# Other queues for three of a stage's stores, and products written over the keys: one step of a hybrid decoder on one core

## The chip, the cores and the metric

The kernel runs on one core of a Trainium2 chip. The time is device microseconds of one execution. Engines are TensorE, VectorE, ScalarE, GpSimd and SyncE; in profile rows they are PE (PEld for its weight loads), DVE, ACT, POOL and SP. A name with a q behind it, as SPq, is the sequencer of that engine, which issues DMAs and waits.

## The reference

One layer for a prompt of 2048 tokens and for 8 samples of 4 new tokens each. The input is normalised and multiplied by one wide matrix; half of the result goes through attention, half through an mLSTM; both are gated and meet in an output matrix. What matters here is the attention of the new tokens, which see a cache of 2048 keys and values per sample in three patterns:

```python
DILATED_PATTERNS = ((128, 1), (512, 4), (2048, 16))      # window, step

def dilated_partial_sample(q, kc, vc, dil, n_back):
    idx = WB + jnp.arange(T)[:, None] - jnp.arange(n_back + 1)[None, :] * dil
    kg, vg = jnp.take(kc, idx, axis=1), jnp.take(vc, idx, axis=1)
    s = jnp.einsum('bthe,btjhe->bthj', q, kg) * (HEAD_DIM_ATT ** -0.5)
    ...
    return m, den, acc
```

and, of the prompt, the rotated keys and the values, which are outputs as they are (`p_win_k`, `p_win_v`), and the queries, keys and values that its own attention reads.

## The kernel before

The work is in three stages. The first projects the prompt, the second runs the prompt's attention from what the first has stored in DRAM (`q_scr`, `k_scr`, `v_scr`), the third runs the mLSTM and the output matrix. The change lies in the first (`phase_a`).

There the prompt is cut in 16 tiles of 128 tokens. For each tile `unit(i, j)` runs five projections of 512 columns: j = 0 queries, 1 keys, 2 values, 3 and 4 gates. Each is 24 matmuls of 128x512 (L165 to L167) into one PSUM tile of four; then ScalarE and VectorE take it out: for j < 3 as a high and a low 16-bit part (`t16`; the low part is L524), with the rotation of queries and keys on VectorE (L518 to L526) and GpSimd (L527 to L530), for keys and values also as 32-bit rows (`kvout`, L523); for the gates as `z` (L504, L505). All of it is stored: `t16` to `q_scr`, `k_scr` or `v_scr` (L533), `kvout` to `p_win_k` or `p_win_v` (L535), `z` to `z_scr` (L506). All these stores are issued by SyncE, as are the loads.

The first four tiles run projection by projection, as the weights come in. From the fifth on, tile by tile, other work is mixed in by its place in the program: preparing later weights (L134 to L148), normalising the next tokens (L215 to L226, stored as `x_scr` by GpSimd, L492), and the samples' attention. Its scores (`SampleAttention.scores`, one call for each of the 8 samples, spread over tiles 4 to 10 by the tuple `SCORES`) go without TensorE: the sample's four queries are replicated over 128 partitions in the tile `d_qb` (one buffer, L372), and for each pattern a = 2, 1, 0 a tile of keys `d_kv` (two buffers) is loaded (L366; L362 for a = 0, which needs one key per partition for all four tokens). For a = 2 and 1 GpSimd multiplies the queries into the key tile (L379), four products of 128x512; for a = 0 VectorE multiplies the keys into the query tile (L381). VectorE reduces each product (L382). After the eighth sample come a softmax (its sum is L401) and the values (L428) on TensorE; their key tiles use the same two buffers, and `d_qb`.

The order on each engine, and on each queue, isn't written out: a planner lays it out at build time from the program's order and a simulated time. An engine runs its instructions in that order, and a wait holds all behind it.

Of the kernel before, what the change touches and what calls it, by code (L numbers as in the profile page):

```python
# [16 lines left out]
ALU = mybir.AluOpType  # L17
# [13 lines left out]
NTOK = 4  # L31
# [122 lines left out]
def token_matmuls(nc, ps, x16, tok, hi, lo, cols):  # L154

    for last in token_steps(nc, ps, x16, tok, hi, lo, cols):
        pass
    return last
# [120 lines left out]
class SampleAttention:  # L279
# [89 lines left out]
    def scores(self, b):  # L369
        G, nc = self.G, self.G.nc  # L370
        qb = self.pool.tile([P, NTOK, 512], F32, tag="d_qb", name="d_qb")
        nc.sync.dma_start(out=qb.rearrange("p t e -> p (t e)"),  # L372
                          in_=G.ds_scr[0].rearrange("(b t) e -> b (t e)", t=NTOK)[b].partition_broadcast(P))
        for a in (2, 1, 0):
            t = self.piece("cache_win_k", b, a)
            for i in range(NTOK):
                p = t[:, i] if a else qb[:, i]
                if a:
                    nc.gpsimd.tensor_tensor(p, p, qb[:, i], ALU.mult)  # L379
                else:  # L380
                    nc.vector.tensor_tensor(p, p, t[:, 0], ALU.mult)  # L381
                nc.vector.tensor_reduce(self.sc[:, a, b, i], p.rearrange("p (h d) -> p h d", d=DA), AX.X, ALU.add)  # L382

    def softmax(self):
# [72 lines left out]
def phase_a(G, I, O):  # L457

    nc, tc = G.nc, G.tc
    wv = I["w_in"].rearrange("(kt p) c -> p kt c", p=P)  # L460
    wo = I["w_out"].rearrange("(kt p) c -> p kt c", p=P)
    with ExitStack() as st:
# [32 lines left out]
        def unit(i, j):  # L495

            x16 = x16s[i // 2]
            tok = slice((i % 2) * P, (i % 2 + 1) * P)
            rows = slice(i * P, (i + 1) * P)
            ps = pp.tile([P, 512], F32, tag="proj", name="ps_proj", bufs=4)  # L500
            pe = token_matmuls(nc, ps, x16, tok, hi[j], lo[j], slice(0, 512))
            if j >= 3:
                z = pool.tile([P, 512], F32, tag="z", name="z", bufs=2)
                nc.scalar.activation(z, ps, AF.Tanh, scale=G.whinv[:, j:j + 1])  # L504
                nc.vector.scalar_tensor_tensor(z, z, 1.0, ps, ALU.add, ALU.mult)  # L505
                nc.sync.dma_start(out=G.z_scr[rows, (j - 3) * 512:(j - 2) * 512], in_=z)  # L506
                return pe
            pv = ps.rearrange("p (h d) -> p h d", d=DA)
            R = 0 if j == 2 else 16
            t16 = v16[i % 2] if j == 2 else pool.tile([P, HA, (2 * DA, 3 * DA)[j]], F16, tag="t16", name="t16", bufs=3)  # L510
            l0 = 66 if j == 2 else DA
            o = pool.tile([P, HA, DA], F32, tag="kvout", name="kvout", bufs=2) if j else None
            if j < 2:
                ra = pool.tile([P, HA, 16], F32, tag="ra", name="ra")
                rb = pool.tile([P, HA, 16], F32, tag="rb", name="rb")
                r = pool.tile([P, HA, 16], F32, tag="rr", name="rr", bufs=2)
                table = lambda c, n: G.rope_p[:, i, c:c + n].unsqueeze(1).broadcast_to([P, HA, n])
                nc.vector.tensor_tensor(ra, pv[:, :, 0:16], table(0, 16), ALU.mult)  # L518
                two = lambda x: x.rearrange("p h (a e) -> p h a e", a=2)
                nc.vector.tensor_tensor(two(rb), two(pv[:, :, 0:16])[:, :, ::-1], two(table(16, 16)), ALU.mult)  # L520
            nc.scalar.activation(t16[:, :, R:DA], pv[:, :, R:], AF.Copy, scale=USC)
            if j:
                nc.scalar.activation(o[:, :, R:], pv[:, :, R:], AF.Copy, scale=G.wainv[:, j:j + 1])  # L523
            nc.vector.scalar_tensor_tensor(t16[:, :, l0 + R:l0 + DA], pv[:, :, R:], USC, t16[:, :, R:DA], ALU.mult, ALU.subtract)  # L524
            if j < 2:
                nc.vector.tensor_tensor(r, ra, rb, ALU.add)  # L526
                nc.gpsimd.tensor_copy(t16[:, :, 0:16], r)  # L527
                nc.gpsimd.tensor_tensor(t16[:, :, DA:DA + 16], r, t16[:, :, 0:16], ALU.subtract)
            if j == 1:
                nc.gpsimd.tensor_scalar(o[:, :, 0:16], r, G.isc[:, 1:2], 0.0, ALU.mult, ALU.add)  # L530
                nc.scalar.activation(t16[:, :, 2 * DA:], t16[:, :, 0:DA], AF.Copy)
            scr = (G.q_scr, G.k_scr, G.v_scr)[j]
            nc.sync.dma_start(out=scr.rearrange("r t e -> t r e")[rows], in_=t16.rearrange("p (r h) e -> p r (h e)", r=4))  # L533
            if j:
                nc.sync.dma_start(out=O["p_win_k" if j == 1 else "p_win_v"][rows, :], in_=o.rearrange("p h d -> p (h d)"))  # L535
            return pe

        def gate_unit(i):
# [43 lines left out]
        for j in range(5):  # L582
            if j < 3:
                wf.append(w_load(j + 2))
            if 0 < j < 4:
                if j == 1:
                    with tc.issue_after(last[DVE]):
                        prepare(j + 1, wf[j + 1])
                else:
                    prepare(j + 1, wf[j + 1])  # L590
            if j == 4:
                weights(G, pool, ginv, weight_loads(G, pool, wv[:, :, 4608:4616], 8), 8, G.gcol, sb=wg)
                xs = pool.tile([P, KT, NS], F32, tag="xs", name="xs")
                nc.sync.dma_start(out=xs, in_=I["xsT"].rearrange("(kt p) t -> p kt t", p=P))
                norm_columns(G, pool, pp, xs, G.xd.rearrange("p k a t -> p a k t"), NS, pool.tile([P, 4, NS], F32, tag="sq2s", name="sq2"), tag="s")
            for i in range(4):
                unit(i, j)
                if j == 4:
                    gate_unit(i)
                    if i == 1:  # L600
                        run(xprep(2))
# [24 lines left out]
        for i in range(4, NT):  # L626
            block = blocks.get(i)
            if block is not None:
                next(block)
            if i % 2 == 0 and i // 2 + 1 < 8:  # L630
                norm = xprep(i // 2 + 1)
                next(norm)
            for j in range(5 if i < NT - LATE else 3):
                pe = unit(i, j)
                if pending is not None and j == 1:
                    behind(pe, pending)
                    pending = None
                if block is not None and j in (0, 3 if i < NT - LATE else 2):
                    behind(pe, block)
                if j == 1 and i // 2 + 1 < 8:  # L640
                    behind(pe, norm)
            gate_unit(i)
            pending = block
            for _ in range(SCORES.count(i)):
                SA.scores(b_next["k"])
                b_next["k"] += 1
            if i == SCORES[-1]:
                SA.softmax()
            for _ in range(VALUES.count(i)):
                SA.values(b_next["v"])  # L650
                b_next["v"] += 1
            if i == VALUES[-1]:
                SA.finish()
# [8 lines left out]
        for n, (i, j) in enumerate(late):  # L662
            unit(i, j)
            if n == 2:
                stacks(G, 0, G.stk, lambda: pp.tile([P, 512], F32, tag="proj", name="ps_k", bufs=4).bitcast(F16))
# [1057 lines left out]
```

## Time and profile before

| | |
|---|---|
| median of 3 runs | 1520.45 us (1520.35 to 1530.15) |
| profiled execution | 1522.74 us |
| its span | 1520.6 us |
| TensorE busy | 1383.7 us (91%) |
| VectorE busy | 982.9 us (65%) |
| ScalarE busy | 737.2 us (48%) |
| GpSimd busy | 467.2 us (31%) |
| mean granted clock of TensorE | 0.97 |

The profile is of one execution. Its span goes from the first instruction to the last; the device time holds 2.1 us more. Matmuls overlap and their ends are modelled, so that a TensorE which is busy is not one at its peak; its idle time, though, is idle. The clock is a share of 2.4 GHz: 1 and 0.5 are its two levels, and a number between them is a mean.

### The profile page before, as it was taken

What the parts mean: (1) busy time and instruction counts of PE and PEld (TensorE: products, weight loads), DVE (VectorE), ACT (ScalarE), POOL (GpSimd) and SP (SyncE); (2) the same over time, 40 slices, a digit from 0 to 9 for tenths busy, and PEclk for the clock granted to TensorE, in tenths of its full rate; (3) what the DMA queues carried; (4) which work ended last, traced back from release to release, by engine and by line L of the source; (5) the groups of instructions that cost most, each with busy time, mean ns of one, the idle gap of its engine ahead of it and who ended that gap; (6) DMA issues with size and microseconds to landing.
All of it is one profiled execution on the core that took longest, in us unless ns stands there. A gap on an engine that the chain in (4) does not pass through costs nothing.

```text
span 1520.6 us, 28991 instructions
## 1 busy us (share of the span) xinstructions
PE 1383.7 (91%) x10679; PEld 856.3 (56%) x10679; DVE 982.9 (65%) x3054; ACT 737.2 (48%) x1685; POOL 467.2 (31%) x797
## 2 busy tenths in 40 slices
PE   4899988989999996999898976879999999999996
PEld 2445444444434346878688844555666666666653
DVE  5763776777643456888686804767666666666665
ACT  5365433454344336878687823334444444444432
POOL 1361334353310013645358932211211111111110
PEclk9999999999999998999999998989999999999999
DMA  8354587868869948977857866452655555553212
GB/s 295 111 181 159 164 279 289 280 217 308 278 213 379 324 136 288 340 220 227 237 173 208 306 234 213 149 174 74 212 160 188 160 187 160 188 160 106 78 48 77
DMA packets 153404, 310.96 MB, mean 204 GB/s; under 512 B 13533, under 2 KB 102782, under 8 KB 142686
## 3 DMA queue, kind: packets, MB, share of 16 engines
q1 hardware_dynamic: 149166, 230.10, 47.6%
q0 software_dynamic: 3952, 78.75, 14.2%
q8 instruction: 84, 1.38, 0.4%
q14 instruction: 58, 0.48, 0.1%
q10 hardware_dynamic: 144, 0.26, 0.0%
HBM read 231.80 MB, written 144.38 MB: 247 GB/s over the span
## 4 chain that ended last, share of the span: by engine, by line
PE 36%; DMA 19%; DVE 13%; ACT 5%; POOL 4%; issue 4%; SPq 1%; POOLq 0%; ACTq 0%; DVEq 0%
DMA Mb<-g_scr 5%; DMA qi<-g_scr 4%; PE ps_t L1052 3%; PE ps_proj L165 3%; PE ps_proj L167 3%; PE ps_proj L166 3%; DVE cd L1194 2%; DMA v<-v_scr 2%; PE ps_out L167 2%; PE ps_out L165 2%; PE ps_out L166 2%; DMA qn<-q_scr 2%; POOL d_kv L379 2%; PE ps_s L1030 2%; PE ps_dv L428 2%
## 5 line engine op out<-in xcount | busy, mean ns | idle before, releaser
L165 PE MATMUL ps_proj<-wa,x 128*128 128x512 f16 x640 | 246.2, 386 | 19.0 <-DVE t L524 10.1
L166 PE MATMUL ps_proj<-wa,x 128*128 128x512 f16 x640 | 246.5, 386 | 2.5 <-POOL wa L111 2.0
L167 PE MATMUL ps_proj<-wa,x 128*128 128x512 f16 x640 | 246.6, 386 | 1.0 <-ACT x L226 1.0
L1039 DVE CUSTOM_DVE_ANT_0 sc<-ps_s,mask,ncqk 128x256 f32<-128x256 f32 (+1 forms) x384 | 142.6, 420 | 25.7 <-PE ps_s L1031 9.0
L1041 POOL TENSOR_SCALAR sc<-sc,o 128x256 f32<-128x256 f32 (+1 forms) x272 | 113.0, 427 | 86.0 <-DVE o L1039 77.4
L165 PEld LDWEIGHTS <-x 128*128 128x128 f16 x768 | 73.8, 99 | 100.5 <-issue 16.9
L1056 DVE SCALAR_TENSOR_TENSOR tl<-ps_t,th 128x512 f16<-128x512 f32 (+1 forms) x152 | 102.4, 680 | 35.9 <-ACT th L1055 35.2
L167 PEld LDWEIGHTS <-x 128*128 128x128 f16 x768 | 73.4, 99 | 85.9 <-issue 12.9
L1194 DVE SCALAR_TENSOR_TENSOR cd<-pre,cw,cd 128x256 f32<-128x256 f32 x168 | 85.2, 512 | 51.9 <-ACT cd L1188 50.0
L166 PEld LDWEIGHTS <-x 128*128 128x128 f16 x768 | 73.4, 99 | 79.4 <-issue 11.4
L379 POOL TENSOR_TENSOR d_kv<-d_kv,d_qb 128x512 f32<-128x512 f32 x64 | 84.6, 1357 | 89.8 <-DMA d_qb<-ds_scr 80.5
L1055 ACT ACTIVATE th<-ps_t 128x512 f16<-128x512 f32 (+1 forms) x152 | 90.4, 595 | 37.2 <-PE ps_t L1052 35.3
L167 PE MATMUL ps_out<-wo,yt 128*128 128x512 f16 x256 | 95.5, 382 | 7.3 <-DVE yt L1291 6.4
L1052 PE MATMUL ps_t<-c_id,pr 128*128 128x128 f32 x600 | 100.3, 288 | 1.7 <-DVE tl L1056 1.4
L165 PE MATMUL ps_out<-wo,yt 128*128 128x512 f16 x256 | 98.0, 383 | 2.2 <-ACT yt L1293 1.1
L166 PE MATMUL ps_out<-wo,yt 128*128 128x512 f16 x256 | 97.8, 382 | 0.0
L1368 POOL TENSOR_TENSOR Mb<-Mb,big 128x512 f32<-128x512 f32 x16 | 20.3, 1269 | 250.1 <-DMA Mb<-g_scr 217.8
L1068 PE MATMUL ps_o<-v,th 128*128 128x65 f16 x600 | 80.6, 195 | 14.0 <-ACT th L1055 10.7
L1174 PE MATMUL ps_qk<-cx,wb 128*128 128x256 f16 x256 | 71.6, 280 | 17.9 <-ACT pre L1184 16.1
L1372 ACT ACTIVATE Mb<-Mb,gcols 128x128 f32<-128x128 f32 x64 | 20.5, 390 | 127.5 <-POOL Mb L1368 127.5
L1367 POOL TENSOR_TENSOR qi<-qi,qk 128x128 f32<-128x128 f32 x60 | 29.8, 523 | 162.9 <-DMA qi<-g_scr 149.0
L1069 PE MATMUL ps_o<-v,th 128*128 128x64 f16 x600 | 79.7, 196 | 0.0
(466 smaller groups left out, 3779.5 us busy)
## 6 DMA issues: line engine op xcount, KB each, us to landing
s_win_k<-cache_win_k POOLq DMA_DIRECT2D x32, 1022.0 KB, 8.2
s_win_v<-cache_win_v POOLq DMA_DIRECT2D x32, 1022.0 KB, 7.9
wf<-w_in SPq DMA_DIRECT2D x18, 1024.0 KB
d_kv<-cache_win_k SPq DMA_DIRECT2D x16, 1024.0 KB
d_kv<-cache_win_v SPq DMA_DIRECT2D x16, 1024.0 KB
A<-att_scr SPq DMA_DIRECT2D x16, 792.0 KB
w_scr<-wst SPq DMA_DIRECT2D x12, 1024.0 KB
att_scr<-o SPq DMA_DIRECT2D x9, 1056.0 KB
```

The source lines that it names most:

```text
L165: nc.tensor.matmul(ps, lhsT=xh, rhs=hi[:, kt, cols], start=kt == 0, stop=False)
L166: nc.tensor.matmul(ps, lhsT=xh, rhs=lo[:, kt, cols], start=False, stop=False)
L167: yield nc.tensor.matmul(ps, lhsT=xl, rhs=hi[:, kt, cols], start=False, stop=kt == KT - 1)
L379: nc.gpsimd.tensor_tensor(p, p, qb[:, i], ALU.mult)
L1039: nc.vector.tensor_tensor_reduce(sc[:, x:x + n], sp[:, x:x + n], G.mask[:, MASK_END[u[0]] - n:MASK_END[u[0]]], G.ncqk, BIG, ALU.add, ALU.m ...
L1041: pooled = nc.gpsimd.tensor_scalar(sc[:, x:x + n], sc[:, x:x + n], -1.0, nm, ALU.mult, ALU.add)
L1052: nc.tensor.transpose(out=tp[:, c * P:(c + 1) * P], in_=pr[:, c * P:(c + 1) * P], identity=G.idf)
L1055: nc.scalar.activation(th[:, :w], tp[:, :w], AF.Copy, scale=PSC)
L1056: nc.vector.scalar_tensor_tensor(tl[:, :w], tp[:, :w], PSC, th[:, :w], ALU.mult, ALU.subtract)
L1068: nc.tensor.matmul(o, lhsT=th[:, cs], rhs=V[:, 0:65], start=first, stop=False)
L1069: nc.tensor.matmul(o[:, 0:64], lhsT=th[:, cs], rhs=V[:, 66:130], start=False, stop=False)
L1194: eng.scalar_tensor_tensor(d, pre[:, j:j + 256], cw[:, ct, j:j + 1], d, ALU.mult, ALU.add)
```

## The change

Two edits. In the scores of the first pattern (a = 0) VectorE's products are written into the key tile instead of the query tile; as all four tokens read the keys of slot 0, the tokens are taken in the order 3, 2, 1, 0, so that slot 0 is overwritten last. The other patterns do the same products as before, in the new order. In `unit`, the store of the queries' `t16` and that of the new keys' rows are issued by GpSimd, and that of the new values' rows by ScalarE; the stores of the keys' and values' `t16` and of the gates stay with SyncE.

```diff
         for a in (2, 1, 0):
             t = self.piece("cache_win_k", b, a)
-            for i in range(NTOK):
-                p = t[:, i] if a else qb[:, i]
-                if a:
-                    nc.gpsimd.tensor_tensor(p, p, qb[:, i], ALU.mult)
-                else:
-                    nc.vector.tensor_tensor(p, p, t[:, 0], ALU.mult)
+            for i in reversed(range(NTOK)):
+                p = t[:, i]
+                (nc.gpsimd if a else nc.vector).tensor_tensor(p, t[:, i if a else 0], qb[:, i], ALU.mult)
                 nc.vector.tensor_reduce(self.sc[:, a, b, i], p.rearrange("p (h d) -> p h d", d=DA), AX.X, ALU.add)
@@ unit @@
             scr = (G.q_scr, G.k_scr, G.v_scr)[j]
-            nc.sync.dma_start(out=scr.rearrange("r t e -> t r e")[rows], in_=t16.rearrange("p (r h) e -> p r (h e)", r=4))
+            (nc.gpsimd if j == 0 else nc.sync).dma_start(out=scr.rearrange("r t e -> t r e")[rows], in_=t16.rearrange("p (r h) e -> p r (h e)", r=4))
             if j:
-                nc.sync.dma_start(out=O["p_win_k" if j == 1 else "p_win_v"][rows, :], in_=o.rearrange("p h d -> p (h d)"))
+                (nc.gpsimd if j == 1 else nc.scalar).dma_start(out=O["p_win_k" if j == 1 else "p_win_v"][rows, :], in_=o.rearrange("p h d -> p (h d)"))
```

## Rows read from the trace of the kernel before

**Rows 1.** Windows, 160 to 400 us: length, busy us of each engine, clock, DMA share, GB/s.

```profile
160.00:400.00 240.00, 225.23 (x1283) 106.91 (x1282) 169.94 (x324) 103.37 (x188) 105.40 (x104) 0.97 0.75 260
```

**Rows 2.** Order of time on TensorE, the six instructions that end its gaps.

```profile
213.60 0.39 PE L165 MATMUL ps_proj<-wa,x 128*128 128x512 f16 x1 [4.17 <-DVE t L524]
...
265.46 0.80 PE L225 MATMUL ps_xt<-idh,xhl 128*128 128x128 f16 x6 [4.71 <-DVE war L97]
...
280.06 0.39 PE L165 MATMUL ps_proj<-wa,x 128*128 128x512 f16 x1 [1.15 <-DVE t L524]
...
342.06 0.61 PE L165 MATMUL ps_proj<-wa,x 128*128 128x512 f16 x1 [4.75 <-DVE t L524]
...
414.54 0.38 PE L165 MATMUL ps_proj<-wa,x 128*128 128x512 f16 x1 [1.69 <-DVE z L505]
...
438.28 0.62 PE L401 MATMUL ps_den<-d_mx,ones 128*32 128x256 f32 x2 [2.61 <-DVE d_mx L399]
```

**Rows 3.** Windows around four of the gaps, same columns.

```profile
209.00:219.00 10.00, 5.83 (x23) 2.14 (x19) 8.72 (x19) 5.76 (x11) 8.66 (x10) 0.83 0.90 307
260.00:271.00 11.00, 6.29 (x35) 3.32 (x34) 7.35 (x16) 2.38 (x5) 9.38 (x8) 0.84 0.58 206
337.00:348.00 11.00, 6.25 (x21) 2.21 (x18) 10.79 (x24) 6.57 (x12) 5.20 (x8) 0.69 0.99 337
...
435.00:445.00 10.00, 7.39 (x52) 2.51 (x49) 5.70 (x15) 3.38 (x8) 0.00 (x0) 0.83 0.45 132
```

**Rows 4.** Order of time on VectorE, around the gap before 342 us.

```profile
317.30 0.66 DVE L505 SCALAR_TENSOR_TENSOR z<-z,ps_proj 128x512 f32<-128x512 f32 x1
...
320.83 0.55 DVE L524 SCALAR_TENSOR_TENSOR t<-ps_proj,t 128x384 f16<-128x384 f32 x1
328.31 0.69 DVE L382 TENSOR_REDUCE d_sc<-d_kv 128x8 f32<-128x512 f32 x1 [6.93 <-POOL d_kv L379]
...
341.46 0.54 DVE L524 SCALAR_TENSOR_TENSOR t<-ps_proj,t 128x384 f16<-128x384 f32 x1
```

**Rows 5.** Waits, 160 to 440 us: total us, times, longest.

```profile
DVE d_sc L382 <- POOL d_kv L379: 48.1, 21, 8.4
...
POOL d_kv L379 <- DMA d_qb<-ds_scr: 80.5, 7, 16.6
```

**Rows 6.** Order of time on VectorE, first pattern's products and reductions of two blocks.

```profile
192.39 0.67 DVE L381 TENSOR_TENSOR d_qb<-d_qb,d_kv 128x512 f32<-128x512 f32 x1
...
311.05 0.67 DVE L381 TENSOR_TENSOR d_qb<-d_qb,d_kv 128x512 f32<-128x512 f32 x1
...
315.23 0.67 DVE L382 TENSOR_REDUCE d_sc<-d_qb 128x8 f32<-128x512 f32 x1
```

**Rows 7.** Order of time on SyncE's queue, issues of the same two blocks.

```profile
195.46 0.33 SPq L372 DMA_DIRECT2D d_qb<-ds_scr  x1
...
311.23 0.88 SPq L366 DMA_DIRECT2D d_kv<-cache_win_k  x2
...
314.44 0.39 SPq L535 DMA_DIRECT2D p_win_v<-kvout  x1
...
316.02 0.37 SPq L372 DMA_DIRECT2D d_qb<-ds_scr  x1
```

**Rows 8.** Order of time on GpSimd, products of the block that follows.

```profile
327.01 11.66 POOL L379 TENSOR_TENSOR d_kv<-d_kv,d_qb 128x512 f32<-128x512 f32 x8 [15.84 <-DMA d_qb<-ds_scr]
```

**Rows 9.** Waits of SyncE's queue, 160 to 440 us: total us, times, longest.

```profile
SPq L362 <- DVE d_sc L382: 44.9, 7, 12.6
```

**Rows 10.** Issues of stores by GpSimd (ns, min/median/max) and one by ScalarE (start us, us).

```profile
L492 POOL DMA_DIRECT2D x_scr<-x x8: 610/626/742, 18.5 to 464.5; - x8
...
L1113 POOL DMA_DIRECT2D att_scr<-o x1: 1232/1232/1232, 879.0 to 879.0; - x1
...
1516.43 0.37 ACTq L1313 DMA_DIRECT2D y_prompt<-early_x  x1
```

**Rows 11.** Order of time on TensorE, the start of the stage.

```profile
83.41 0.38 PE L166 MATMUL ps_proj<-wa,x 128*128 128x512 f16 x1 [2.01 <-POOL wa L111]
```

## Prediction

> **What bounds the kernel now.** The change lies in the first stage, so I read a window of it first: from 160 to 400 us TensorE is busy 225.2 of 240 us, VectorE 169.9, and ScalarE and GpSimd 103 to 105; the DMA has a share of 0.75 [rows 1]. The reader is to see two things there: the stage is TensorE's, and some 15 us of it are not used, while all others have room. Only what shortens TensorE's idle time can show in the end.
>
> Next come TensorE's gaps from 160 to 445 us, each told by the instruction that ends it [rows 2]: six gaps, 4.17 + 4.71 + 1.15 + 4.75 + 1.69 + 2.61 = 19.1 us. Behind four of them the granted clock is at its lower level (1.2 of 2.4 GHz) for a while: the windows around them have a mean of 0.83, 0.84, 0.69 and 0.83 over 10, 11, 11 and 10 us [rows 3]. A mean of 0.83 over 10 us costs 1.7 us of work; that makes 1.7 + 1.8 + 1.7 = 5.2 us, and of the third window's 3.4 us I count 2.4, since TensorE stood for part of that time anyway. 19.1 + 7.6 = 26.7 us, 1.75% of the time, is all that this stretch can give: the ceiling of the change.
>
> Then one gap followed back, in VectorE's order of time [rows 4]. It finishes a gate at 317.96, evacuates a query unit until 321.38, and then stands 6.93 us until the first reduction of a key product (L382) at 328.31; the evacuation that TensorE needs (L524) comes at 341.46, and TensorE resumes at 342.06. The reduction waited for GpSimd's product, and that for the queries replicated over the partitions (d_qb): these waits add up to 48.1 us on VectorE and, at one a block of scores, 80.5 us on GpSimd [rows 5]. So: late d_qb, late products, VectorE stands in its order, PSUM is not emptied, TensorE stops.
>
> Why is d_qb late? It has one buffer. In the old code the first pattern's products overwrite it, so it is free only after their last reduction: 315.23 + 0.67 = 315.90, while the last product ended at 311.05 + 0.67 = 311.72 [rows 6]. Its load is issued at 316.02, behind two key loads at 311.23 on the same queue [rows 7], and GpSimd starts at 327.01 [rows 8], 11 us after the issue.
>
> **The change, part by part.**
>
> *Products over the key tile.* Instructions, shapes and count stay. What moves is the release: d_qb is free after the last product, 316.02 - 311.72 = 4.3 us before its issue of today in the block shown, and 2.4 us in the first block (192.39 + 0.67 = 193.06 against 195.46) [rows 6, 7]. The price goes to the key buffer of the first pattern, now held through the last reduction. That buffer takes the next block's second key load, which GpSimd needs only after four products: eight take 11.66 us, so 5.8 us after its start [rows 8]. That cover is enough; were it gone, the 3.5 us between last product and last reduction would come back as a wait of GpSimd. The order on SyncE should also turn round: today both key loads (1 MB each) go ahead of d_qb; afterwards the second becomes free last and goes behind it. At the 260 GB/s of this stretch [rows 1] 1 MB is 4 us; I take between 0 and 4 for it. So d_qb lands 2.4 to 8 us earlier a block; I take 4.5, nearer to the release alone, because the new queue order is inferred and not seen.
>
> *The reversed order of the four tokens* is needed because the last product overwrites its own input. It costs nothing: no instruction is added, and all four read the same tile on one engine.
>
> *48 stores leave SyncE.* One takes 0.39 us of issue there [rows 7], and, more important, they stand among loads: SyncE stood 44.9 us in seven waits for a key buffer (L362), with whatever comes next kept behind [rows 9]. In the block shown a value store at 314.44 is issued shortly before d_qb, at a time at which d_qb was not yet free; today the release, not the issue, is last. When the release moves forward, such stores are what is late next, 0.4 us each and what they wait for. Taking them away keeps the gain whole; by itself I cost it at 0 to 1 us a block.
>
> *16 value stores on ScalarE.* A store on that queue takes 0.37 us [rows 10]; 16 x 0.37 = 6 us beside an engine that is busy 103 of 240 us [rows 1]. The data come from ScalarE's own instruction just before, so there is no new wait. Nothing of it lies on TensorE's path; if an issue stood still for long, the gate activations behind it would be late.
>
> *32 stores on GpSimd.* The nearest rows are 0.63 us for a 1 MB store of this stage and 1.23 us for one with many short runs [rows 10]. A query store has four short runs per partition, one of new keys a single long run, so 0.7 us is nearest; 32 x 0.7 = 22 us, with ends of 20 and 39, on an engine that is idle for half of the stage [rows 1]. The query store is issued while GpSimd would stand for d_qb anyway: the unit's low part is done at 321.38 [rows 4], the products start at 327.01 [rows 8]. Cost there 0. In the start it is not covered: at 83.41 TensorE waited 2.01 us for GpSimd's low part of the value weights [rows 11], and four key stores now fall into that work, 4 x 0.63 = 2.5 us. I take half, 1.3 us, with ends of 0 and 4.9 (1.23 each).
>
> The Trainium skill, *SBUF — State Buffer*, in its account of the ports, warns of this part: GpSimd writes the descriptors of the DMAs it issues, and a VectorE operation that holds the shared port keeps it from doing so. No row here shows it. If it held for each store, the part would cost more than taken here, and the rival on GpSimd's order would be likelier.
>
> **The sum**, gap by gap. The first gap (4.17, and 1.7 of clock): d_qb lands 2.4 to 6 us earlier, so 3.5 come back. The one of 4.71 (and 1.8): the advance is carried over from block to block, since the chain of scores doesn't wait for TensorE; 5. The one of 1.15: all. The one of 4.75 (and 2.4): 6. The one of 1.69 ends with a gate's evacuation on the same engine: 1. The one of 2.61 waits for the softmax maximum (L399), behind the scores' end, and I leave it: 0. Together 16.65; less 1.3 at the start; less 2, an estimate of one gap of the smaller size shown, because VectorE's order is laid out anew and some evacuation will stand behind a reduction again. That is 13.3 us, with ends of 0 and 26.7. The profiled execution took 1522.7 us (span 1520.6), 2.3 more than the median of the runs: 1522.7 - 13.3 = 1509.4, and from the median 1520.45 - 13.3 = **1507**. The later stages start at the end of this one and keep their length.
>
> **The rivals.**
>
> *Nearly all comes back* (0.13): d_qb lands 7 to 8 us early, and the softmax, which starts with the last scores, moves forward too: 22 to 27 us, 1494 to 1499. For it speaks that VectorE's wait of 6.93 us [rows 4] is shorter than that advance; against it the start and the new order.
>
> *It hardly does what it says* (0.30): products and reductions alternate in the program, and if VectorE's order puts the last product right before the last reduction, d_qb is released one reduction, 0.67 us, earlier instead of 2.4 to 4.3: seven blocks x 0.67 = 4.7 us. The same comes out if the DMA is what d_qb waits for, since its bytes stay: three stores of 256 KB then run beside d_qb and not behind it, 0.75 MB at 260 GB/s = 3 us, which eats most of the release. Either way 1512 to 1520. Against the first speaks the block shown, with 3.5 us between last product and last reduction; against the second that 0.75 of the DMA is used [rows 1].
>
> The Trainium skill, *DMA: Bandwidth & Descriptors*, under "Issuing engines are not separate DMA queues", says that issuing from several engines saves only the sequencer's time, usually little. By that the moved stores are worth next to nothing, as costed above, and 1507 rests on the buffer alone.
>
> *GpSimd's order turns against it* (0.12), the slower end: a query store waits for VectorE's low part and stands ahead of the eight products. Today the low part is 327.01 - 321.38 = 5.6 us ahead of the products; once d_qb gains more than that, the store holds them and not the load. It ends slower when two stores a block stand between the landing and the products at the upper price, 2 x 1.23 = 2.5 us beyond today's start: 7 x 2.5 = 17 us on TensorE, 1538.
>
> **How the numbers follow.** The forecast (0.45) covers 1500 to 1513. The range reaches down to the near-full return and up past no change: 1495 to 1524 leaves about 0.1 on either side. A change of under 1%, 15 us, is about what can't be told from none here; 1505.2 cuts the forecast's case a little past its middle: faster 0.13 + 0.25 = 0.38, slower 0.10, the same 0.52.
>
> **What would show it.** In the new profile the load of d_qb should be issued within 1 us of the last product and ahead of the second key load; VectorE's waits for GpSimd's products should fall from 48.1 to under 25 us; TensorE's gaps from 19.1 to some 7. It would be wrong by: the same seven waits of over 10 us for d_qb; query stores right ahead of the products with idle time before them; a longer wait for the value weights near 83 us; or an order that moves stages after 445 us.

## The result and the profile after

The changed kernel takes 1532.9 us (median of 20 runs, 1523.3 to 1540.6) and the kernel before 1524.2 us (20 runs on the same chip, 1516.1 to 1532.4). The ratio is 1.0057, with a 95% interval of 1.0040 to 1.0075: slower by 8.7 us, where 1507 was forecast and 1524 was the upper end of the range. The forecast started from a median of three, 1520.45; from the 1524.2 of these 20 the same gain would give 1511. The profiled execution took 1529.9 us, with a span of 1528.1 and a mean granted clock of 0.968. In the changed file all lines from the scores on have numbers lower by 3: products L378, reductions L379, a unit's evacuations L515 to L521, a gate's L502.

I follow the signs that the prediction named. First the release, in the block that [rows 6 to 8] show for the kernel before (the sixth load of d_qb): the first pattern's last product on VectorE, then the issues on SyncE's queue, then GpSimd's products.

```profile
293.44 0.68 DVE L378 TENSOR_TENSOR d_kv<-d_kv,d_qb 128x512 f32<-128x512 f32 x1
...
294.15 0.33 SPq L372 DMA_DIRECT2D d_qb<-ds_scr  x1
295.14 0.33 SPq L366 DMA_DIRECT2D d_kv<-cache_win_k  x1
...
304.04 11.29 POOL L378 TENSOR_TENSOR d_kv<-d_kv,d_qb 128x512 f32<-128x512 f32 x8 [5.17 <-DMA d_qb<-ds_scr]
```

The load of d_qb is issued 0.03 us after the last product ends (294.12), in this block as in all seven, and ahead of the second key load. GpSimd's products start 9.9 us after the issue here, against 11.0 before [rows 7, 8]; over the seven blocks it is 4.8 to 9.9 us (median 5.7) against 9.6 to 16.5 (median 10.9). This part does what the prediction said. The waits from 160 to 440 us (total us, times, longest) shrink:

```profile
POOL d_kv L378 <- DMA d_qb<-ds_scr: 58.0, 7, 18.0
...
DVE d_sc L379 <- POOL d_kv L378: 27.2, 26, 6.6
...
DVE d_kv L378 <- DMA d_kv<-cache_win_k: 14.3, 5, 6.7
```

VectorE waits 27.2 us for products instead of 48.1 (under 25 was the sign), and GpSimd 58.0 instead of 80.5 for d_qb [rows 5]. Of its seven waits three are over 10 us; in the kernel before it was four, not all seven as the prediction has it. The third line has grown: VectorE now waits 14.3 us for first-pattern keys, whose buffer is held longer. In the kernel before it was this:

```profile
DVE d_qb L381 <- DMA d_kv<-cache_win_k: 2.5, 1, 2.5
```

And yet TensorE's gaps are not gone. They are at other places (order of time on TensorE; the bracket is the idle time and what ended it):

```profile
197.36 0.61 PE L225 MATMUL ps_xt<-idh,xhl 128*128 128x128 f16 x8 [2.06 <-DVE war L97]
...
263.05 1.01 PE L225 MATMUL ps_xt<-idh,xhl 128*128 128x128 f16 x8 [6.43 <-DVE war L97]
...
323.02 0.61 PE L225 MATMUL ps_xt<-idh,xhl 128*128 128x128 f16 x8 [1.06 <-DVE war L97]
...
338.19 0.47 PE L165 MATMUL ps_proj<-wa,x 128*128 128x512 f16 x1 [3.21 <-DVE t L521]
...
354.63 0.38 PE L165 MATMUL ps_proj<-wa,x 128*128 128x512 f16 x1 [3.62 <-DVE z L502]
...
394.22 1.06 PE L398 MATMUL ps_den<-d_mx,ones 128*32 128x256 f32 x2 [3.85 <-DVE d_mx L396]
...
521.90 2.07 PE L425 MATMUL ps_dv<-d_kv,d_sc 128*32 128x512 f32 x12 [1.95 <-DMA d_kv<-cache_win_v]
...
553.29 0.94 PE L688 MATMUL ps_k<-idh,kn 128*128 128x128 f16 x8 [3.32 <-DVE z L502]
```

The first six make 20.2 us, where the six of before made 19.1 [rows 2]; the last two lie in a stretch (445 to 561 us) in which the kernel before had no idle time. The softmax sum (L398) comes at 394 us instead of 438 [rows 2], so the chain of scores ends 44 us earlier. The stage's last matmul of L165 starts at 571.2 us, before at 560.4: the 10.8 us lie here, and some 3 are won back later (the span grew by 7.5).

The largest gap, read in VectorE's order of time, says why:

```profile
249.89 0.69 DVE L379 TENSOR_REDUCE d_sc<-d_kv 128x8 f32<-128x512 f32 x1 [1.12 <-POOL d_kv L378]
...
254.31 0.68 DVE L502 SCALAR_TENSOR_TENSOR z<-z,ps_proj 128x512 f32<-128x512 f32 x1
255.23 0.69 DVE L379 TENSOR_REDUCE d_sc<-d_kv 128x8 f32<-128x512 f32 x1 [0.24 <-POOL d_kv L378]
256.45 0.69 DVE L379 TENSOR_REDUCE d_sc<-d_kv 128x8 f32<-128x512 f32 x1 [0.54 <-POOL d_kv L378]
257.68 0.69 DVE L379 TENSOR_REDUCE d_sc<-d_kv 128x8 f32<-128x512 f32 x1 [0.54 <-POOL d_kv L378]
258.69 1.93 DVE L378 TENSOR_TENSOR d_kv<-d_kv,d_qb 128x512 f32<-128x512 f32 x3 [0.32 <-DMA d_kv<-cache_win_k]
260.54 1.27 DVE L379 TENSOR_REDUCE d_sc<-d_kv 128x8 f32<-128x512 f32 x2
...
262.12 0.67 DVE L379 TENSOR_REDUCE d_sc<-d_kv 128x8 f32<-128x512 f32 x1
262.72 0.28 DVE L97 TENSOR_REDUCE war<-ps_am 128x1 f32<-128x128 f32 x1
```

TensorE wants the small reduction L97, of 0.28 us. Between it and the gate's evacuation before it now stand six score reductions and three products, and the first three go at GpSimd's pace, one every 1.22 us. In the order of before, at the same L97, two reductions stood there. Compared instruction by instruction, the new order moves 174 of 2670 instructions on VectorE (by up to 48 places; readings of an accumulator left out) and 145 of 10208 on TensorE (by up to 256); counted are the fewest that have to move to turn one order into the other.

**Theories.** *Order theory*: the release is worth what was forecast, but the planner, with d_qb free earlier, lays VectorE's reductions ahead of evacuations, and this gives the gain back. *Stores theory*: the 48 moved stores cost what the release wins. *Key-buffer theory*: holding the first pattern's key tile makes its next load late, and that is the loss.

### The profile page after: what moved, and what is told of

Its sections match the earlier page's. It is cut to its first block, busy times and chain, and to the rows that moved or that the text cites. A ratio compares the mean times of both kernels' runs of the same rounds, so it can differ in the third digit from the quotient of the medians.

```text
span 1528.1 us, 28970 instructions
## 1 busy us (share of the span) xinstructions
PE 1385.6 (91%) x10679; PEld 855.1 (56%) x10679; DVE 984.8 (64%) x3054; ACT 738.0 (48%) x1685; POOL 482.4 (32%) x829
## 4 chain that ended last, share of the span: by engine, by line
PE 39%; DMA 25%; DVE 19%; ACT 7%; POOL 4%; issue 3%; SPq 2%; DVEq 0%; POOLq 0%; ACTq 0%
DMA Mb<-g_scr 4%; PE ps_proj L165 4%; PE ps_proj L167 4%; PE ps_proj L166 4%; PE ps_t L1049 4%; DMA qi<-g_scr 3%; DMA d_kv<-cache_win_k 3%; DVE cd L1191 3%; PE ps_out L167 3%; DMA d_qb<-ds_scr 3%; PE ps_out L165 2%; PE ps_out L166 2%; DMA kn<-k_scr 2%; POOL d_kv L378 2%; DVE d_sc L379 2%
## 5 line engine op out<-in xcount | busy, mean ns | idle before, releaser
L165 PE MATMUL ps_proj<-wa,x 128*128 128x512 f16 x640 | 246.3, 387 | 14.4 <-ACT wa L559 4.1
L165 PEld LDWEIGHTS <-x 128*128 128x128 f16 x768 | 73.7, 99 | 94.2 <-issue 18.1
L378 POOL TENSOR_TENSOR d_kv<-d_kv,d_qb 128x512 f32<-128x512 f32 x64 | 84.1, 1344 | 65.4 <-DMA d_qb<-ds_scr 58.0
L165 PE MATMUL ps_out<-wo,yt 128*128 128x512 f16 x256 | 97.8, 382 | 2.2 <-ACT yt L1290 1.1
L1065 PE MATMUL ps_o<-v,th 128*128 128x65 f16 x600 | 80.4, 195 | 14.3 <-ACT th L1052 11.3
L1171 PE MATMUL ps_qk<-cx,wb 128*128 128x256 f16 x256 | 70.9, 277 | 18.6 <-ACT pre L1181 16.1
L518 ACT ACTIVATE t<-ps_proj 128x384 f16<-128x384 f32 x32 | 15.6, 488 | 144.6 <-DVE rb L517 115.6
L379 DVE TENSOR_REDUCE d_sc<-d_kv 128x8 f32<-128x512 f32 x96 | 64.0, 678 | 27.5 <-POOL d_kv L378 27.2
```

The costliest lines, as they stand in the source:

```text
L165: nc.tensor.matmul(ps, lhsT=xh, rhs=hi[:, kt, cols], start=kt == 0, stop=False)
L378: (nc.gpsimd if a else nc.vector).tensor_tensor(p, t[:, i if a else 0], qb[:, i], ALU.mult)
L1065: nc.tensor.matmul(o, lhsT=th[:, cs], rhs=V[:, 0:65], start=first, stop=False)
```

## The experiments

A written order is made so that the queues of the four computing engines run the instructions of another build in its order: the list of instruction numbers of each engine is stored in the kernel, and each instruction is made to follow its predecessor without a semaphore. DMA issues aren't in the lists: on every queue, the moved stores on GpSimd's and ScalarE's included, the planner places them.

```
+def written_order(G):
...
+    for packed in ORDER.values():
+        last = None
+        for n in array.array("i", zlib.decompress(base64.b85decode(packed))):
...
+                if last is not None:
+                    G.tc.add_manual_dep(i, last.name, dep, reason="written_order")
...
+        written_order(G)
```

All ratios are against the kernel before, on the same chip, with their 95% intervals; microseconds are differences of the medians.

**Control: the kernel before with its own order written out.**

> A control: the kernel before, its own order written out as a list and nothing else changed. Every theory expects 0, within 3 us either way; were it 5 us or more, the two kernels with a written order would have to be read against this one and not against the kernel before.

Measured: 0.9999 (0.9983 to 1.0016). Writing the order out costs nothing that can be told.

**The whole change in the order of before.**

> The whole change, but TensorE, VectorE, ScalarE and GpSimd run their instructions in the order of the kernel before; only the queues and the tile that the products overwrite differ. Order theory: the release stays and nothing is shifted, -5 to -13 us. Stores theory: the stores are still there, +3 to +15 us. Key-buffer theory: the hold is still there, +3 to +10 us.

Measured: 0.9901 (0.9866 to 0.9935), -14.3 us, just beyond the range of the order theory, where the other two expected a loss. The same instructions, queues and buffers as in the changed kernel, 24 us faster than it (1.0057 / 0.9901 = 1.016). In its profile TensorE has two gaps of over 1 us from 160 to 445 us (5.3 us; 8.6 with all shorter ones), and in VectorE's order L97 stands behind two reductions:

```profile
275.40 0.61 PE L165 MATMUL ps_proj<-wa,x 128*128 128x512 f16 x1 [2.68 <-DVE t L521]
...
427.66 0.77 PE L398 MATMUL ps_den<-d_mx,ones 128*32 128x256 f32 x2 [2.60 <-DVE d_mx L396]
```

```profile
251.93 0.67 DVE L502 SCALAR_TENSOR_TENSOR z<-z,ps_proj 128x512 f32<-128x512 f32 x1
256.95 0.69 DVE L379 TENSOR_REDUCE d_sc<-d_kv 128x8 f32<-128x512 f32 x1 [4.34 <-POOL d_kv L378]
258.18 0.69 DVE L379 TENSOR_REDUCE d_sc<-d_kv 128x8 f32<-128x512 f32 x1 [0.54 <-POOL d_kv L378]
...
259.18 0.28 DVE L97 TENSOR_REDUCE war<-ps_am 128x1 f32<-128x128 f32 x1
```

Its waits, same view as above:

```profile
DVE d_kv L378 <- DMA d_kv<-cache_win_k: 17.0, 6, 6.4
...
DVE d_sc L379 <- POOL d_kv L378: 14.0, 15, 4.3
```

VectorE's wait for products is at 14.0 us, from 48.1 [rows 5], while the wait for first-pattern keys is 17.0, longer than in the changed kernel, in a kernel that is 1% faster than before. The key-buffer theory falls as the cause.

**The kernel before in the order of the changed one.**

> The kernel before, with none of the change, but its four engines run their instructions in the order of the changed kernel. Order theory: the scores stand earlier in the order than the late d_qb allows, so +9 us at least and up to +30. Stores theory and key-buffer theory: neither a store nor a buffer is touched, so 0 to +3 us.

Measured: 1.0209 (1.0175 to 1.0243), +32.8 us, just above the range given. Two of its gaps on TensorE, at the place where the changed kernel has 6.43 us:

```profile
264.12 1.01 PE L225 MATMUL ps_xt<-idh,xhl 128*128 128x128 f16 x8 [7.39 <-DVE gates L542]
...
272.28 1.01 PE L225 MATMUL ps_xt<-idh,xhl 128*128 128x128 f16 x8 [6.72 <-DVE war L97]
```

Together with the two kernels and the run above this is a table of two by two: in the old order the change gives 0.990, in the new one 1.0057 / 1.0209 = 0.985. The code is better in either order, by 15 to 23 us; the new order costs 1.6% with the new code and 2.1% with the old.

**The score edit alone, planner's order.** The diff is that of the scores; the two store lines stay as before.

> The score edit alone; all stores stay on SyncE's queue. Order theory (the planner lays the four engines' order anew once the products release d_qb earlier, and the new order gives the gain back): the order is new here too, so -3 to +10 us against the kernel before. Stores theory (the 48 moved stores cost what the release wins): the gain shows bare, -8 to -15 us. Key-buffer theory (the first pattern's key tile is held longer, so its next load is late): +3 to +10 us, since the hold is all that is left.

Measured: 1.0053 (1.0031 to 1.0075), +7.6 us: as slow as the whole change, with no store moved. Its order differs from that of before by 113 instructions on TensorE and 167 on VectorE, and its softmax sum starts at 392.8 us: the score edit by itself makes the planner lay out the new order. Whether it does so by the earlier release or by the reversed tokens, which are one edit here, was not tried.

**The score edit alone, in the order of before.**

> The score edit alone, in the order of the kernel before; all stores stay on SyncE's queue. Order theory, by the prediction's terms: the release is the whole gain and the stores cost or save at most 1 us a block, so -6 to -15 us, within 5 us of the whole change in the old order (-14). Stores theory in its weaker form (the stores cost something that the old order hides): 3 us or more better than the whole change in the old order. If SyncE's queue is what is late next: 3 to 8 us worse than it.

Measured: 0.9870 (0.9841 to 0.9900), -19.3 us: the fastest median of the study, ahead of both kernels, and 4 us beyond the range of the order theory. Only one gap over 1 us is left on TensorE from 160 to 445 us (1.52), and its last matmul of L165 starts at 535.7 us, against 560.4 in the kernel before. It is 5 us better than the whole change in that order, as the stores theory in its weaker form has it, but the intervals overlap.

**The stores alone, planner's order.**

> The 48 moved stores alone; the products still overwrite d_qb. Order theory: the order moves less (33 of TensorE's instructions against 145 in the whole change), so -3 to +4 us. Stores theory: +8 to +20 us. Key-buffer theory: 0, since no tile is held longer.

Measured: 1.0010 (0.9988 to 1.0032): no difference that can be told.

**The stores alone, in the order of before.**

> The 48 moved stores alone, in the order of the kernel before; the products still overwrite d_qb. Order theory: d_qb is released as late as before, so 0 to -5 us, the rest of what the whole change gains in the old order going to the score edit. Stores theory: +3 to +10 us.

Measured: 1.0060 (1.0039 to 1.0082), +8.7 us. So the moved stores cost something after all, and the stores theory holds for a part: here the planner's own order (the run above) is the better one by 7 us. It isn't always the new order that loses.

**TensorE alone in the order of before; VectorE alone in it.** Both have the whole change, and one engine's list each.

> The whole change with TensorE alone in the order of the kernel before (softmax sum and values where they were); VectorE, ScalarE and GpSimd are laid out by the planner and come close to the changed kernel's. If it is VectorE's order (reductions ahead of evacuations) that gives the gain back: +3 to +15 us against the kernel before, as the change. If it is TensorE's own order (softmax sum 44 us earlier, values stretched): -5 to -14 us, as with all four engines in the old order.

> The whole change with VectorE alone in the order of the kernel before; the planner lays out the rest around it, 33 of TensorE's instructions elsewhere than before. If VectorE's order carries the loss, as the +4 us with TensorE alone held suggests: -8 to -16 us, near the -14 with all four engines held. If the loss needs TensorE's or ScalarE's order too: -5 to +5 us.

Measured: TensorE alone 1.0025 (1.0002 to 1.0048), +5.1 us, VectorE alone 0.9890 (0.9864 to 0.9917), -15.9 us. With TensorE's list the gap at L97 is still there; this profile is of the one execution of twelve, 1517.7 us, that lies apart from the others (1533.6 to 1541.4):

```profile
266.99 1.01 PE L225 MATMUL ps_xt<-idh,xhl 128*128 128x128 f16 x8 [7.52 <-DVE war L97]
```

With VectorE's list the gain is that of all four lists. What gave it back goes with VectorE's order; TensorE's 44 us earlier softmax sum is at most a small part. The run doesn't part VectorE from the others wholly: around its list the planner lays them out nearly as before (33 instructions elsewhere on TensorE, not 145; 8 on ScalarE, where the change moves 33).

**Which store.** The score edit in the order of before, with only some of the stores moved; the edits are of this form:

```
-            nc.sync.dma_start(out=scr.rearrange("r t e -> t r e")[rows], ...
+            (nc.scalar if j == 0 else nc.sync).dma_start(out=scr.rearrange("r t e -> t r e")[rows], ...
...
-                nc.sync.dma_start(out=O["p_win_k" if j == 1 else "p_win_v"][rows, :], ...
+                nc.scalar.dma_start(out=O["p_win_k" if j == 1 else "p_win_v"][rows, :], ...
```

All 48 on ScalarE:

> The score edit in the old order with the same 48 stores moved off SyncE, but all of them to ScalarE's queue and none to GpSimd's. With the stores left on SyncE this order gave -19 us, with the change's queues -14. If GpSimd's issuing is what costs the 5 us: -17 to -22 us. If it is the leaving of SyncE's queue (the stores run beside the loads and not behind them): -12 to -16 us, as with the change's queues. If ScalarE's gate work behind a waiting store decides: -5 to -12 us.

Measured: 0.9909 (0.9886 to 0.9932), -13.9 us, as with the change's queues.

New keys alone, `(nc.gpsimd if j == 1 else nc.sync)` in the second line:

> The score edit in the old order with the 16 stores of new keys alone on GpSimd's queue. If these stores, issued among GpSimd's weight products in the first 160 us, are what stretches VectorE's weight operation there (4.9 us in the two kernels with moved stores and the old order, 1.6 at most with the stores on SyncE) and costs the 5 us: -13 to -16 us. If not: -17 to -21 us.

Measured: 0.9906 (0.9885 to 0.9927), -14.0 us.

New keys from the fifth token tile on, `(nc.gpsimd if j == 1 and i >= 4 else nc.sync)`:

> The score edit in the old order with the stores of new keys on GpSimd from the fifth token tile on; those of the first four, which fall among GpSimd's weight products, stay on SyncE. If the stretched weight operation in the start is the whole cost: -18 to -21 us, and no VectorE operation of L113 over 1.7 us before 120 us. If the cost lies later, in the stage of the scores: -13 to -16 us.

Measured: 0.9871 (0.9835 to 0.9906), -17.6 us, just outside both ranges; no operation of L113 is over 1.7 us before 120 us.

Queries alone, `(nc.gpsimd if j == 0 else nc.sync)` in the first line:

> The score edit in the old order with the 16 query stores alone on GpSimd's queue, at 0.8 us each ahead of the products. If they hold the products: -11 to -16 us. If they lie in GpSimd's wait for d_qb, as the prediction has it: -18 to -22 us, and GpSimd's wait for d_qb is shorter by what they take.

Measured: 0.9868 (0.9846 to 0.9889), -18.7 us. GpSimd's wait for d_qb isn't shorter, though: 53.2 us from 160 to 440, against 53.0 with no store moved.

Values alone, `(nc.scalar if j == 2 else nc.sync)` in the second line:

> The score edit in the old order with the 16 value stores alone on ScalarE's queue. If the new keys on GpSimd are what costs: -18 to -21 us, as with all stores on SyncE. If it is any store that leaves SyncE's queue with keys or values: -13 to -16 us.

Measured: 0.9886 (0.9852 to 0.9921), -16.0 us, at the end of the second range.

And two without the score edit, in the order of before. New keys on GpSimd:

> The kernel before in its own order with the 16 stores of new keys alone on GpSimd. If these carry the cost of the moved stores: +5 to +10 us, as with all 48. If not: -2 to +3 us.

Measured: 1.0030 (1.0002 to 1.0059), +5.7 us.

Queries on GpSimd and values on ScalarE:

> The kernel before in its own order with the query stores on GpSimd and the value stores on ScalarE, the new keys left on SyncE. If the new keys carry the cost: -3 to +2 us. If the other two do: +5 to +10 us.

Measured: 1.0024 (0.9997 to 1.0051), +4.7 us, between the two ranges. The last two add up to 0.54%, beside the 0.60% of all 48, but with intervals of nearly 0.3% on either side these times don't part the stores. What the runs do part: the query stores on GpSimd have no cost that can be told beside the score edit (0.9868 against 0.9870 with none moved). All on ScalarE is no better than with GpSimd, so GpSimd's issuing alone isn't the price.

For the new keys the traces show a place, VectorE's weight operations in the first 120 us (ns, min/median/max), with the stores on GpSimd throughout:

```profile
L113 DVE SCALAR_TENSOR_TENSOR wa<-wf,wsc,wa x23: 735/751/4911, 24.3 to 113.9; 128x512 f16<-128x512 f32 x23
```

and with those of the first four token tiles left on SyncE:

```profile
L113 DVE SCALAR_TENSOR_TENSOR wa<-wf,wsc,wa x23: 737/752/1649, 24.4 to 112.3; 128x512 f16<-128x512 f32 x23
```

Windows from 86 to 122 us of the same two kernels, columns as in [rows 1]:

```profile
86.00:122.00 36.00, 33.90 (x150) 14.94 (x149) 23.93 (x30) 17.99 (x29) 20.17 (x21) 0.95 0.50 154
```

```profile
86.00:122.00 36.00, 35.61 (x168) 16.20 (x165) 16.12 (x32) 15.61 (x26) 18.82 (x20) 1.00 0.52 162
```

In the first VectorE is busy 23.9 us, in the second 16.1, with 30 and 32 instructions. TensorE stands 2.1 us instead of 0.4 (1.82 of them at 101.85 us, until an evacuation of VectorE), and its mean clock is 0.95 instead of 1.00, which is 1.8 us of work: 3.5 us together. All profiles bear this out. From the start of the eleventh projection to that of the sixteenth pass 30.3 to 31.3 us in the four kernels that have the order of before and the new keys' stores on GpSimd from the start, and 26.1 to 26.9 us in every other kernel, those with the same stores in another order among them. So 4 to 5 us of the moved stores' price in the order of before lie here, and this is most of the 7 us between the stores alone in that order and in the planner's. What the stores cost after the start, as with all on ScalarE (26.1 us here, and yet 5 us behind the score edit alone), stays open, and by the intervals it may be nothing.

## Why the prediction was wrong, step by step

**What bounds the kernel** held. The stage is TensorE's, its gaps are ended by VectorE, and VectorE stands for late products: when the release came forward with the four engines' order held, the gaps of 160 to 445 us fell from 19.1 [rows 2] to 8.6 us (whole change, order of before; 5.3 in gaps of over 1 us), where some 7 were expected.

**Products over the key tile** held, the size roughly. The load went out right after the last product and ahead of the second key load. From the end of the last product to GpSimd's next products passed 12.3 to 19.8 us in the kernel before and 7.2 to 16.6 in the whole change in the order of before: 4.6 us less on the mean of seven blocks, where 4.5 were taken. The gap-by-gap 16.65 us stand beside 19.3 us measured for the score edit alone in the old order; and that sum less 1.3 at the start, 15.35, beside 14.3 for the whole change in it. That the second is so near is partly luck: the release gave some 3 us more than the sum had, and the stores took some 5 where 1.3 was taken. The rival *nearly all comes back* was nearest to the score edit by itself: in its one profile the first stage ends 24.7 us earlier, near the ceiling of 26.7.

**The step that failed** is the term "less 2, an estimate of one gap of the smaller size shown, because VectorE's order is laid out anew and some evacuation will stand behind a reduction again". The mechanism named there is the one found; its size was taken from one small gap, and it measured 24 us (1.016), more than the whole gain. Two things were missed in sizing it. The sum was made on the order of before, as though each gap kept its place and only shrank; but the score edit alone has the planner lay out the chain of scores anew, with its softmax sum 45 us earlier (392.8 us against 438.3). That the planner does so for the earlier release, which its simulated time would hold, is inferred. And a reduction that is placed early doesn't cost its own 0.67 us: it holds VectorE until GpSimd's product is there, one every 1.22 us, so that three of them ahead of an evacuation cost 3.7 us of VectorE's queue. The warning of the prediction's end, "an order that moves stages after 445 us", came true too (the gaps of 1.95 and 3.32 us). Why the planner takes the reductions for ready that early was not measured.

**The moved stores** were taken at 0 to 1 us a block of gain and 1.3 us of price. In the old order the price is 8.7 us alone (1.0060) and some 5 us beside the score edit, the latter within what the intervals leave open. The start, where half of the price of the key stores was expected, holds 4 to 5 us of it, at the upper end that was given (4.9), though by another mechanism than GpSimd's delay: near 82 us TensorE's wait for GpSimd's part (2.01 us in [rows 11]) became shorter, 1.73 us in the changed kernel and 1.2 in the four that pay the price; what is late there is VectorE. The Trainium skill, *DMA: Bandwidth & Descriptors*, "Issuing engines are not separate DMA queues", would make the moved stores worth little; the runs agree that there was nothing to win by them.

**The reversed order of the tokens** was not tried by itself; the score edit includes it and is faster in the order of before.

**The rivals.** *It hardly does what it says* gave 1512 to 1520 and has the sign wrong: the release did come forward. *GpSimd's order turns against it* was the one on the slower side, for a store ahead of the products; the run with the query stores on GpSimd shows none of it. The slower end came by an order, as that rival said, but by VectorE's.

## What to carry to other kernels

Where a planner lays out the engines' order from a simulated time, a change to when a buffer comes free is two changes: the release, and a new order; price the second by the whole gain that it can take back, not by one gap. Test them apart by running the new code in the old order and the old code in the new one: here 0.990 and 1.021 against 1.006 for both. If the old order with the new code wins, keep that order; with VectorE's list alone the gain was there.

## What the runs showed of the hardware

In the first 120 us a weight operation of VectorE (L113, median 0.75 us) took 4.9 us in all four kernels that had the order of before and the new keys' stores on GpSimd from the start, at most 1.73 us in the others that had that order for all four engines, and at most 3.1 us in the four that had these stores and another order. The kernel with the key stores alone, VectorE and GpSimd by time:

```profile
78.87 4.91 DVE L113 SCALAR_TENSOR_TENSOR wa<-wf,wsc,wa 128x512 f16<-128x512 f32 x1
78.98 1.36 POOL L110 TENSOR_SCALAR wf<-wf,wsc 128x512 f32<-128x512 f32 x2
80.31 2.26 POOL L111 TENSOR_TENSOR wa<-wf,wa 128x512 f16<-128x512 f32 x2
...
82.56 0.69 POOL L110 TENSOR_SCALAR wf<-wf,wsc 128x512 f32<-128x512 f32 x1
```

The same place where the first stores stay on SyncE:

```profile
78.67 1.91 POOL L110 TENSOR_SCALAR wf<-wf,wsc 128x512 f32<-128x512 f32 x2
78.67 1.23 DVE L113 SCALAR_TENSOR_TENSOR wa<-wf,wsc,wa 128x512 f16<-128x512 f32 x1
```

In the first, VectorE's operation lasts through five operations of GpSimd that run at their shorter times (0.68 us for an L110) and ends 0.5 us after the last of them; in the second the two engines slow each other (0.96 us for an L110) and VectorE is through in 1.23 us. The Trainium skill, *SBUF — State Buffer*, "Who interferes with whom", describes a pair of ports shared by the two as a lock, held for one instruction, with the loser waiting until it ends. The first trace agrees in that GpSimd kept its shorter times while VectorE stood, but here the loser waited through five instructions in a row. What decides which of the two happens was not settled: a store a microsecond earlier goes before it in the first, but the kernels with these stores in another order have it too, without the 4.9 us. The prediction had weighed that page the other way round, with GpSimd as the one that is held up.

Soon after, in the first kernel, three more of VectorE's operations take 9.12 us (read on VectorE alone):

```profile
86.23 9.12 DVE L113 SCALAR_TENSOR_TENSOR wa<-wf,wsc,wa 128x512 f16<-128x512 f32 x3
```
